# Products by token in groups of 512 columns, with quarter-of-rows weight tiles and one PSUM bank for each block, in one decoder-layer step on Trainium2

## The chip, the cores and the metric

The kernel runs on one core of one Trainium2 chip. The metric is the time of one execution on the device in microseconds, as the median of several runs. The kernel before takes 4701.04 us (median of three runs, 4698.99 to 4721.07 us).

## The reference

One decoder layer is computed for a prompt of 1024 tokens and, with the same weights, for one new token of each of 8 samples. Everything is float32 and the model width is 1024. Cut to what matters here:

```python
proj = h @ w_in                                  # h = RMSNorm(x), (tokens, 1024)
z, xbc, dt_raw, rw, gate_raw = split(proj)       # z: 1024 columns, gate_raw: 2 x 1024
y_ssd  = rmsnorm(SSD(xbc, dt_raw) * silu(z))
y_rwkv = RWKV7(rw)
merged = sigmoid(gate_ssd) * y_ssd + sigmoid(gate_rwkv) * y_rwkv
x = x + merged @ w_out
x = x + CrossAttn(rmsnorm(x)) @ w_mo             # 4 heads, 256 memory tokens
x = x + PEER(rmsnorm(x))                         # 8 heads x top 16 of 16384 one-neuron experts
y = rmsnorm(x)
```

PEER finds, for every token, 8 x 16 experts: scores by `w_pq` and sub-keys, a top 16 of each half, a top 16 of their pairs. Each chosen expert costs a row of 4 KB of `expert_u` (a dot product with the token) and a row of `expert_v` (added with a coefficient).

## The kernel before

**Fronts and experts.** The 1024 prompt tokens go in four groups of two blocks of 128 tokens. All of the layer but the experts' sums is a "front" of a group (`front(gi)`, `gi` 0 to 3; "front 1" to "front 4" in the text). Eight sample rows ride along as a small third block: their input products in front 1, their Z, gate and `w_out` products in front 2, their `w_mo` product and expert choice in front 3. The experts of one group are worked on beside the next front: for each of the 128 choices of a block, POOL gathers 128 rows into a `U` tile (L1512, 512 KB) and DVE takes the dot product (L1516) or adds the row to the sum (L1568). After front 4 come what is left of these, the last group's `u` rows, and a dense sum over `expert_v` for two blocks (matmuls with `cs`, `vs` and `cmat`).

**Order.** A scheduler places the instructions of all engines when the kernel is built. A front's instructions stand ahead of the previous group's experts, which fill in. On the chip each engine runs its own list in that fixed order, and SP issues the loads in a fixed order too, each once its buffer is free.

**Two forms of product.** By channel: weights stationary, tokens moving (`by_channel`). By token: a block's activations stationary (`hT`, `mT`, `oT`: 8 slices of 128 rows), weights moving, the result a block's rows by some columns (`by_token`). The change is about four products by token, each to 1024 columns: Z (L499 on: `w_in` columns, evicted by ACT `Tanh` into an `f2` tile at L507 and by DVE into `mg` at L509, and at L511 and L512 for the sample rows), the SSD gate GS (L847 on: ACT L854, DVE L855), and `project` for `w_out` and `w_mo` (L1042 on: DVE L1053). The RWKV gate GR that follows GS also goes by token and isn't touched. Front 1 does its products in a three-part split for accuracy (`sa`), so its Z and GS aren't touched either; its `project` is, and there `rest` runs once for each block.

**As it is before,** each of the four goes in steps of 256 columns: `weights()` loads two `w` tiles (rows 0 to 511 and 512 to 1023, 512 KB each, in runs of 1 KB), and then for each block a `pp` bank takes 8 matmuls of 256 columns and is evicted before the next but one block can use it. All matmuls are recorded at the helper L112; one float32 matmul of the program leaves two records.

**Buffers.** PSUM has eight banks of 512 columns: `pp` 2, `pc` 2, `pg` 1, `tp` 1, `pv` 2. `pc` is also used by the PEER scores (product of queries and sub-keys, evicted by ACT into one of three `sc` tiles, which DVE's top 16 frees), by the SSD, by the scan and by the attention of the samples. `w` has 5 tiles, `f2` has 4.

**Neighbours.** Z is followed by `dt` and by the 12 convolution channels, GS and GR run beside DVE's triangular inverse (L841 and L843), which the scan needs, and each `project` is followed by an RMSNorm.

Of the kernel before, what the change touches and what calls it, by code (L numbers as in the profile page):

```python
# [13 lines left out]
OP = mybir.AluOpType  # L14
# [30 lines left out]
def decode_layer(ctx, tc, I, O):  # L45
# [289 lines left out]

    kt2_d = dr.tile([2, P, 8, P], F32, name="kt2_d")
# [125 lines left out]
    def front(gi):  # L462
# [36 lines left out]
        for i in range(4):  # L499
            wt = weights(w_in, Z0 + i * 256, split=sa)  # L500
            aside_satt(SATT[0])
            s2 = slice(i * 256, i * 256 + 256)
            for b, (t0, n) in enumerate(body):
                p = pp()
                by_token(wt, hT, t0, n, p)
                th = f2()
                S.activation(th[:n, :256], p[:n, :256], AF.Tanh, scale=0.5)  # L507
                if b < nb:
                    V.scalar_tensor_tensor(mg[b][:n, s2], th[:n, :256], 1.0, p[:n, :256], op0=OP.add, op1=OP.mult)  # L509
                else:  # L510
                    V.scalar_tensor_tensor(th[:n, :256], th[:n, :256], 1.0, p[:n, :256], op0=OP.add, op1=OP.mult)  # L511
                    V.tensor_tensor(mg[b][:n, s2], th[:n, :256], mg[b][:n, s2], op=OP.mult)  # L512
# [334 lines left out]
        for i in range(4):  # L847
            wt = weights(w_in, GS0 + i * 256, split=sa)
            s2 = slice(i * 256, i * 256 + 256)
            for b, (t0, n) in enumerate(body):  # L850
                p = pp()
                by_token(wt, hT, t0, n, p)
                th = f2()
                S.activation(th[:n, :256], p[:n, :256], AF.Tanh, scale=0.5)  # L854
                V.scalar_tensor_tensor(mg[b][:n, s2], th[:n, :256], 1.0, mg[b][:n, s2], op0=OP.add, op1=OP.mult)  # L855
# [178 lines left out]
        def rest(bl):  # L1034
# [7 lines left out]
            def project(w, src, smp_src=None):  # L1042

                for i in range(4):
                    wt = weights(w, i * 256)
                    s2 = slice(i * 256, i * 256 + 256)
                    for b, (t0, n) in enumerate(body):
                        p = pp()
                        if b == nl and smp_src:
                            by_token(wt, smp_src, 0, n, p)  # L1050
                        else:
                            by_token(wt, src, t0, n, p)
                        V.tensor_tensor(mg_[b][:n, s2], p[:n, :256], mg_[b][:n, s2], op=OP.add)  # L1053
# [749 lines left out]
```

## Time and profile before

| | |
|---|---|
| median of three runs | 4701.04 us |
| the profiled execution | 4729.15 us, span 4727.4 us |
| PE busy, DVE busy | 75%, 78% |
| ACT busy, POOL busy | 29%, 53% |
| 16 DMA engines busy | 56.0% gathers, 26.5% all other loads and stores |
| granted TensorE clock, mean | 0.795 of full speed |

Busy times are those of one profiled execution. A window of the trace gives, for a stretch of the span, each engine's busy time, the granted TensorE clock (1.0 is 2.4 GHz, 0.5 is 1.2 GHz) and the busy share of the DMA engines. "[x <-y]" behind a row is the idle time of the engine before it and what ended it. PE busy counts pipelined matmuls and isn't PE at its peak.

### The profile page before, as it was taken

Reading aid. Unit: us, or ns where it says so; the run is one execution under the profiler, and the core shown is the slowest. Engines: PE = TensorE matmul, PEld = TensorE weight load, DVE = VectorE, ACT = ScalarE, POOL = GpSimd, SP = SyncE. Lnnn points to the kernel's source line nnn. Section 1 sums busy time; section 2 is a strip of 40 time slices with the busy share of each in tenths; the row PEclk is TensorE's granted clock in tenths of the full one; section 3 lists DMA queues with packets and bytes.
Section 4 is the critical chain, followed back from the end, with each engine's and each line's share of the span. In section 5 each row is a group of like instructions: output and inputs, shape, how many; then the busy total and the mean of one; then the engine's idle time right before and its main releaser. Section 6 shows DMA issues by size and latency. Waiting matters only on the chain.

```text
span 4727.4 us, 56327 instructions
## 1 busy us (share of the span) xinstructions
PE 3534.4 (75%) x18278; PEld 2706.4 (57%) x18278; DVE 3697.7 (78%) x7765; ACT 1351.2 (29%) x3489; POOL 2501.9 (53%) x2059
## 2 busy tenths in 40 slices
PE   7889875779886786788785884387976885338998
PEld 6778764557565565366574673265655743235555
DVE  5662287998878679988886699888766797998888
ACT  5545322133123221133132221132222215233322
POOL 0000035665656645564666657855545477774664
PEclk9987877888865887788757886588757897559999
DMA  4342588899978998899989987899869878988998
GB/s 123 99 130 73 173 280 318 269 320 344 337 260 283 354 339 275 318 323 318 349 269 353 340 280 272 281 328 312 287 217 357 310 239 312 344 311 326 406 406 352
DMA packets 609103, 1369.20 MB, mean 290 GB/s; under 512 B 86124, under 2 KB 332296, under 8 KB 608800
## 3 DMA queue, kind: packets, MB, share of 16 engines
q0 software_dynamic: 260352, 948.03, 56.0%
q1 hardware_dynamic: 348456, 417.57, 26.5%
q8 instruction: 145, 2.38, 0.2%
q14 instruction: 150, 1.23, 0.1%
HBM read 1335.60 MB, written 29.90 MB: 289 GB/s over the span
## 4 chain that ended last, share of the span: by engine, by line
DVE 32%; PE 30%; DMA 15%; issue 12%; ACT 5%; POOL 5%; SPq 1%; another core or an unknown queue 0%; POOLq 0%; DVEq 0%; ACTq 0%
PE pp L112 16%; DVE U L1516 10%; PE pc L112 8%; DVE acc L1568 5%; POOL U L1512 4%; DMA U<-in_expert_v_dram,idx 4%; DMA U<-in_expert_u_dram,idx 3%; PE pg L112 2%; PE pv L112 2%; DVE q3b L450 2%; DMA w<-in_w_in_dram 1%; PE tp L112 1%; DMA q<-kt_d 1%; DVE vs L1616 1%; DVE f L579 1%
## 5 line engine op out<-in xcount | busy, mean ns | idle before, releaser
L1512 POOL DMA_INDIRECT U<-in_expert_u_dram,idx x1024 | 1298.6, 1268 | 732.4 <-issue 189.8
L1516 DVE CUSTOM_DVE_ANT_0 U<-U,xa 128x1024 f32<-128x1024 f32 x1032 | 1267.9, 1239 | 115.3 <-DMA U<-in_expert_u_dram,idx 106.5
L1512 POOL DMA_INDIRECT U<-in_expert_v_dram,idx x768 | 925.8, 1205 | 724.7 <-DVE acc L1568 183.1
L1568 DVE SCALAR_TENSOR_TENSOR acc<-U,cf,acc 128x1024 f32<-128x1024 f32 x708 | 924.0, 1305 | 98.6 <-DMA U<-in_expert_v_dram,idx 85.1
L112 PE MATMUL pp<-qw,w 128*128 128x256 f32 (+2 forms) x2872 | 745.8, 413 | 151.2 <-issue 40.9
L112 PEld LDWEIGHTS pp<-qw,w 128*128 128x128 f32 x2872 | 591.3, 218 | 277.1 <-issue 110.8
L112 PE MATMUL pp<-w,qw 128*128 128x256 f32 (+1 forms) x2528 | 633.9, 405 | 117.9 <-DVE g L509 30.0
L112 PEld LDWEIGHTS pp<-w,qw 128*128 128x128 f32 (+1 forms) x2528 | 484.5, 195 | 247.2 <-DVE g L509 34.1
L112 PE MATMUL pc<-vs,cs 128*128 128x512 f32 x510 | 200.1, 447 | 35.8 <-ACT vs L118 19.9
L112 PE MATMUL pp<-q,w 128*128 128x128 f32 (+1 forms) x1024 | 196.0, 350 | 16.6 <-DMA w<-in_w_pq_dram 8.8
L112 PEld LDWEIGHTS pp<-q,w 128*128 128x128 f32 x1024 | 169.1, 210 | 33.0 <-ACT q L118 10.5
L121 POOL TENSOR_TENSOR q3b<-q3b,q3b 128x400 f32<-128x400 f32 (+1 forms) x130 | 154.6, 1202 | 57.3 <-DVE q3b L450 55.1
L112 PE MATMUL pp<-vs,cs 128*128 128x512 f32 x510 | 172.9, 393 | 0.0
L112 PE MATMUL pc<-rst,q 64*64 64x64 f32 x1024 | 170.5, 305 | 1.6 <-issue 1.0
L112 PE MATMUL pg<-q,q 64*128 64x128 f32 (+1 forms) x384 | 108.5, 441 | 79.5 <-DMA q<-kt_d 39.9
L304 PE MATMUL tp<-ident,g 128*128 128x128 f32 (+1 forms) x296 | 62.2, 346 | 138.5 <-DVE g L1018 52.2
L112 PE MATMUL pc<-g,q 128*64 128x64 f32 x1024 | 138.8, 316 | 16.2 <-issue 12.4
L112 PEld LDWEIGHTS pc<-vs,cs 128*128 128x128 f32 x510 | 93.5, 188 | 91.0 <-ACT vs L118 36.2
L112 PEld LDWEIGHTS pg<-q,q 64*128 64x128 f32 (+1 forms) x384 | 81.6, 273 | 101.0 <-DMA q<-kt_d 42.6
L112 PE MATMUL pc<-q,q 64*128 64x128 f32 (+1 forms) x512 | 102.1, 343 | 47.7 <-ACT q L118 27.8
L304 PEld LDWEIGHTS tp<-ident,g 128*128 128x128 f32 (+1 forms) x296 | 44.0, 183 | 157.3 <-issue 55.9
L112 PEld LDWEIGHTS pc<-rst,q 64*64 64x64 f32 x1024 | 114.4, 188 | 29.9 <-issue 3.2
(506 smaller groups left out, 6336.6 us busy)
## 6 DMA issues: line engine op xcount, KB each, us to landing
w<-in_w_in_dram SPq DMA_DIRECT2D x248, 512.0 KB
U<-in_expert_v_dram SPq DMA_DIRECT2D x128, 512.0 KB
w<-in_w_pq_dram SPq DMA_DIRECT2D x80, 512.0 KB
w<-in_w_out_dram SPq DMA_DIRECT2D x40, 512.0 KB
w<-in_w_mq_dram SPq DMA_DIRECT2D x40, 512.0 KB
w<-in_w_mo_dram SPq DMA_DIRECT2D x40, 512.0 KB
U<-in_expert_u_dram,idx POOLq DMA_INDIRECT x1024
U<-in_expert_v_dram,idx POOLq DMA_INDIRECT x768
```

The costliest lines, as they stand in the source:

```text
L112: T.matmul(out, a, b, start=first, stop=last)
L121: G.tensor_tensor(out, a, b, op=op)
L304: T.transpose(p[:, j * P:j * P + n], x[:, c * P:(c + 1) * P], ident[:n, :n])
L450: V.tensor_tensor(oh[:n], iota50[:n, None, :].to_broadcast([n, 8, NCAND]), posf[:n, h, k8].unsqueeze(2).to_broadcast([n, 8, NCAND]), op=OP ...
L579: V.scalar_tensor_tensor(acc[:, 3 - k:TP], p[:, :TP - 3 + k], cw(k), acc[:, 3 - k:TP], op0=OP.mult, op1=OP.add)
L1512: G.indirect_dma_start(out=dst, out_offset=None, in_=table, in_offset=bass.IndirectOffsetOnAxis(ap=idx, axis=0))
L1516: V.tensor_tensor_reduce(out=u, in0=u, in1=x, scale=1.0, scalar=0.0, op0=OP.mult, op1=OP.add, accum_out=out)
L1568: V.scalar_tensor_tensor(z["acc"], v, cf, z["acc"], op0=OP.mult, op1=OP.add)
L1616: V.tensor_scalar(rb[:, a, :], iota, by[:, 1, t0 + a:t0 + a + 1], by[:, 2, t0 + a:t0 + a + 1], op0=OP.is_equal, op1=OP.mult)
```

## The change

`wide_by_token` is new. It goes over the weights in four tiles of 256 rows by 512 columns (512 KB, runs of 2 KB), and with each tile does two matmuls of 512 columns for every block; the sums of the blocks stand side by side, one bank for each: `pp` for the first block, `pc` for the second, `pg` for the third. After the fourth tile all blocks are evicted, 512 columns at a time. `project` uses it in all four fronts, Z and GS in fronts 2 to 4.

```diff
+    def wide_by_token(w, c0, body, src, p):
+        for i in range(4):
+            x = wtile().rearrange("p a b -> p (a b)").rearrange("p (k c) -> p k c", k=2)
+            load(x, w[i * 256:(i + 1) * 256, c0:c0 + 512].rearrange("(k p) c -> p k c", p=P))
+            for b, (t0, n) in enumerate(body):
+                for k in range(2):
+                    mm(p[b][:n, :], src(b)[i][:, k, t0:t0 + n], x[:, k, :], i == 0 and k == 0, i == 3 and k == 1)
...
-        for i in range(4):
-            wt = weights(w_in, Z0 + i * 256, split=sa)
-            aside_satt(SATT[0])
-            s2 = slice(i * 256, i * 256 + 256)
-            for b, (t0, n) in enumerate(body):
-                p = pp()
-                by_token(wt, hT, t0, n, p)
-                th = f2()
-                S.activation(th[:n, :256], p[:n, :256], AF.Tanh, scale=0.5)
...
+        def by_512(c0):
+            for i in range(2):
+                ps = [(pp, pc, pg)[b]() for b in range(len(body))]
+                wide_by_token(w_in, c0 + i * 512, body, lambda b: hT, ps)
+                for b, (t0, n) in enumerate(body):
+                    yield b, n, slice(i * 512, i * 512 + 512), ps[b][:n, :]
+        tokens = by_256 if sa else by_512
+        aside_satt(SATT[0])
+        for b, n, s2, p in tokens(Z0):
+            th = f2()[:n, :s2.stop - s2.start]
+            S.activation(th, p, AF.Tanh, scale=0.5)
+            if b < nb:
+                V.scalar_tensor_tensor(mg[b][:n, s2], th, 1.0, p, op0=OP.add, op1=OP.mult)
...
+        for b, n, s2, p in tokens(GS0):
+            th = f2()[:n, :s2.stop - s2.start]
+            S.activation(th, p, AF.Tanh, scale=0.5)
+            V.scalar_tensor_tensor(mg[b][:n, s2], th, 1.0, mg[b][:n, s2], op0=OP.add, op1=OP.mult)
...
             def project(w, src, smp_src=None):
-                for i in range(4):
-                    wt = weights(w, i * 256)
...
+                for i in range(2):
+                    s2 = slice(i * 512, i * 512 + 512)
+                    ps = [(pp, pc, pg)[b]() for b in range(len(body))]
+                    wide_by_token(w, i * 512, cols, lambda b: parts[b], ps)
                     for b, (t0, n) in enumerate(body):
+                        V.tensor_tensor(mg_[b][:n, s2], ps[b][:n, :], mg_[b][:n, s2], op=OP.add)
```

`by_256` is the old loop, kept for front 1. `SATT[0]` is 0, so the moved call does nothing.

## Rows read from the trace of the kernel before

**Rows 1.** The page: engines (us, share, instructions) and DMA queues (packets, MB, share)

```profile
PE 3534.4 (75%) x18278; PEld 2706.4 (57%) x18278; DVE 3697.7 (78%) x7765; ACT 1351.2 (29%) x3489; POOL 2501.9 (53%) x2059
...
q0 software_dynamic: 260352, 948.03, 56.0%
q1 hardware_dynamic: 348456, 417.57, 26.5%
```

**Rows 2.** The page: the chain that ended last, by engine

```profile
DVE 32%; PE 30%; DMA 15%; issue 12%; ACT 5%; POOL 5%; SPq 1%; another core or an unknown queue 0%; POOLq 0%; DVEq 0%; ACTq 0%
```

**Rows 3.** Windows: length, busy us by engine, granted clock, DMA share, GB/s

```profile
1786.00:1872.00 86.00, 55.01 (x219) 45.81 (x219) 82.93 (x253) 12.12 (x27) 53.46 (x46) 0.73 0.81 268
1872.00:2022.00 150.00, 112.17 (x284) 59.54 (x282) 138.56 (x436) 18.80 (x59) 81.40 (x69) 0.75 0.88 315
2767.00:2850.00 83.00, 63.06 (x255) 52.20 (x256) 78.16 (x264) 16.80 (x42) 47.58 (x44) 0.82 0.79 268
2850.00:3002.00 152.00, 49.88 (x141) 36.94 (x140) 144.82 (x418) 19.66 (x47) 117.39 (x85) 0.65 0.80 274
1214.00:1335.00 121.00, 103.33 (x461) 69.21 (x460) 109.31 (x206) 16.80 (x44) 83.17 (x64) 0.90 0.96 347
...
1481.00:1578.00 97.00, 63.76 (x314) 43.74 (x310) 78.14 (x112) 24.35 (x77) 69.29 (x56) 0.79 0.95 341
...
668.00:697.00 29.00, 18.26 (x74) 14.68 (x72) 29.00 (x69) 1.50 (x3) 10.31 (x4) 0.81 0.79 250
```

**Rows 4.** Who waited for whom, whole span: us in total, times, longest

```profile
PE pp L112 <- DVE g L509: 35.9, 14, 6.9
...
PE pp L112 <- ACT f L854: 27.6, 6, 10.3
...
PE pp L112 <- DVE g L1053: 21.9, 10, 4.7
```

**Rows 5.** DVE groups by shape: busy us, mean ns of one, idle before

```profile
L668 DVE TENSOR_TENSOR st<-pp,st 128x512 f32<-128x512 f32 x16 | 10.9, 681 | 0.0
...
L1053 DVE TENSOR_TENSOR g<-pp,g 128x256 f32<-128x256 f32 x64 | 26.8, 420 | 54.8 <-PE pp L112 44.5 <-DMA g<-in_x_prompt_dram 8.1 <-issue 2.1
L509 DVE SCALAR_TENSOR_TENSOR g<-f,pp 128x256 f32<-128x256 f32 x32 | 13.0, 409 | 4.3 <-ACT f L507 4.2
```

**Rows 6.** Timeline of PE: start us, length us, what, records

```profile
683.63 6.62 PE L112 MATMUL pp<-w,qw 128*128 128x256 f32 x16 [3.13 <-DVE g L1053]
...
1786.91 7.07 PE L112 MATMUL pp<-w,qw 128*128 128x256 f32 x32
...
4439.62 0.59 PE L112 MATMUL pp<-U,cmat 128*128 128x512 f32 x1
4440.05 1.02 PE L112 MATMUL pc<-U,cmat 128*128 128x512 f32 x2
```

**Rows 7.** Windows at the start (mostly runs of 1 KB) and at the end (4 KB)

```profile
0.00:250.00 250.00, 204.50 (x1397) 179.56 (x1398) 148.07 (x294) 130.85 (x312) 9.64 (x48) 0.92 0.38 108
...
4500.00:4727.00 227.00, 199.45 (x690) 126.50 (x688) 195.43 (x264) 65.14 (x132) 122.12 (x97) 0.97 0.96 378
```

**Rows 8.** Timeline of PE and ACT: scores of fronts 2 and 3 in `pc`

```profile
1781.40 0.49 PE L112 MATMUL pc<-q,q 128*128 128x128 f32 x2 [0.60 <-ACT gate L456]
...
1870.65 0.38 ACT L118 ACTIVATE sc<-pc 128x256 f32<-128x256 f32 x1 [1.44 <-DVE q3b L424]
...
2849.39 0.37 ACT L118 ACTIVATE sc<-pc 8x256 f32<-8x256 f32 x1 [1.95 <-DVE q3b L424]
```

**Rows 9.** The inverse (fronts 2, 4: first and last start), and GR's last products

```profile
L843 DVE TENSOR_TENSOR g<-g,f x31: 185/354/450, 1255.2 to 1317.5; 128x31 f32<-128x31 f32 x2, 128x60 f32<-128x60 f32 x2, 128x87 f32<-128x87 f32 x2, 128x112 f32<-128x112 f32 x2
...
L843 DVE TENSOR_TENSOR g<-g,f x31: 191/353/426, 3298.5 to 3350.5; 128x31 f32<-128x31 f32 x2, 128x60 f32<-128x60 f32 x2, 128x87 f32<-128x87 f32 x2, 128x112 f32<-128x112 f32 x2
...
1330.58 3.62 PE L112 MATMUL pp<-w,qw 128*8 128x256 f32 x16
...
3346.36 3.62 PE L112 MATMUL pp<-w,qw 128*128 128x256 f32 x16
```

More of the change, by code (lines that the diff above doesn't have):

```diff
@@ L497, in aside_satt, with by_256 @@
                 next(satt)
-        for i in range(4):
-            wt = weights(w_in, Z0 + i * 256, split=sa)
-            aside_satt(SATT[0])
-            s2 = slice(i * 256, i * 256 + 256)
-            for b, (t0, n) in enumerate(body):
-                p = pp()
-                by_token(wt, hT, t0, n, p)
-                th = f2()
-                S.activation(th[:n, :256], p[:n, :256], AF.Tanh, scale=0.5)
[L508 to L512, printed above, removed]
+        def by_256(c0):
+            for i in range(4):
+                wt = weights(w_in, c0 + i * 256, split=True)
+                for b, (t0, n) in enumerate(body):
+                    p = pp()
+                    by_token(wt, hT, t0, n, p)
+                    yield b, n, slice(i * 256, i * 256 + 256), p[:n, :256]
+        def by_512(c0):
+            for i in range(2):
+                ps = [(pp, pc, pg)[b]() for b in range(len(body))]
+                wide_by_token(w_in, c0 + i * 512, body, lambda b: hT, ps)
+                for b, (t0, n) in enumerate(body):
+                    yield b, n, slice(i * 512, i * 512 + 512), ps[b][:n, :]
[6 more added lines that the diff above has]
+                V.scalar_tensor_tensor(mg[b][:n, s2], th, 1.0, p, op0=OP.add, op1=OP.mult)
+            else:
+                V.scalar_tensor_tensor(th, th, 1.0, p, op0=OP.add, op1=OP.mult)
+                V.tensor_tensor(mg[b][:n, s2], th, mg[b][:n, s2], op=OP.mult)
         dtt = t("dtt", [P, 4, 16], 2)
@@ L1042, in project @@
             def project(w, src, smp_src=None):
-                for i in range(4):
-                    wt = weights(w, i * 256)
-                    s2 = slice(i * 256, i * 256 + 256)
-                    for b, (t0, n) in enumerate(body):
[L1048 to L1053, printed above, removed]
+                parts = [smp_src if b == nl and smp_src else src for b in range(len(body))]
+                cols = [(0 if b == nl and smp_src else t0, n) for b, (t0, n) in enumerate(body)]
+                for i in range(2):
+                    s2 = slice(i * 512, i * 512 + 512)
+                    ps = [(pp, pc, pg)[b]() for b in range(len(body))]
+                    wide_by_token(w, i * 512, cols, lambda b: parts[b], ps)
+                    for b, (t0, n) in enumerate(body):
+                        V.tensor_tensor(mg_[b][:n, s2], ps[b][:n, :], mg_[b][:n, s2], op=OP.add)
             mT = [qw() for _ in range(4)]
```

8 lines of the change are left out of this document (removed).

## The prediction

> **What bounds the kernel now.** I read the page first. No engine is full: DVE 78%, PE 75%, and the two DMA queues together hold the 16 DMA engines for 82.5% of the span [rows 1]. The chain of waits is spread in the same way, DVE 32%, PE 30%, DMA 15% [rows 2]: the bound changes from stage to stage. So I cut windows around the four changed products [rows 3]. Two kinds appear. Around GS and GR (1214 to 1335) and `w_out` (1481 to 1578) the DMA engines are busy for 0.96 and 0.95: gathers and weights fill them. Where Z runs in fronts 3 and 4, with the convolutions behind it (1786 to 2022, 2767 to 3002), DVE is busy for 82.93 of 86.00, 138.56 of 150.00, 78.16 of 83.00 and 144.82 of 152.00 us, 92 to 96%, because the last front's top 16 and the experts run beside the new front. Only front 1, which has few experts beside it yet, is held by its own chain of products and evictions; in its window (668 to 697) DMA is at 0.79, and PE works 18.26 of 29.00 us. In the first kind a PE that waits less mostly leaves the transfers as they are, in the second it leaves DVE as it is. That decides how much of each saving below I count.
>
> **The change part by part.** It covers Z and GS in fronts 2 to 4 (7 blocks each) and `project` in all fronts (9 blocks for `w_out`, 9 for `w_mo`): 32 blocks by 1024 columns.
>
> *PE's columns: nothing.* 32 records of 256 columns take 7.07 us; with the last one's tail as long as in the single row below (0.59 less the pitch of 0.43, so 0.16), that is (7.07 - 0.16) / 32 = 0.216 us each. Two more records of 512 columns lengthen a run from 0.59 to 1.02, 0.43 for the second [rows 6]. Twice 0.216 is 0.43: half the weight loads go, but they lay under the matmuls. Bounds: 0, and 0.002 x 1024 new records, 2 us. I take 0.
>
> *Loads: -8 us.* 128 loads stay 128 of 512 KB, 67.1 MB, in runs of 2 KB instead of 1 KB. The gather queue (4 KB rows) takes 0.560 x 4727.4 / 948.03 = 2.79 us of all 16 engines for a MB, the other queue, mostly 1 KB, 0.265 x 4727.4 / 417.57 = 3.00 [rows 1]. If 2 KB came as cheap as the gathers, 67.1 x 0.21 = 14 us. The farthest rows give more: 0.38 x 250 / 27.0 = 3.52 us for a MB in the first window and 0.96 x 227 / 85.8 = 2.54 in the last [rows 7], so at most 67.1 x 0.98 = 66; the least is 0, as a run of twice the length isn't dearer by the byte in any row. I take 14, as those rows are of whole queues. Only 72 of the 128 loads (GS, and `project` of fronts 2 to 4) lie where DMA is full: 14 x 72 / 128 = 8. By the Trainium skill ("DMA: Bandwidth & Descriptors", "Why small descriptors are slow") each packet has some three cycles beside one cycle for 32 bytes: 67 instead of 70 cycles for 2 KB, an estimate of 4% or 9 us of the 201 that 67.1 MB cost, and 5 of them counted; the rows lie above that.
>
> *Fewer evictions: -5 us.* DVE's 132 operations of 256 columns become 66 of 512. One of 256 takes 0.409 to 0.420 us, one of 512 out of PSUM 0.681 [rows 5]: 66 x (0.84 - 0.68) = 10 us of DVE time. Bounds 0 and 10; DVE is full for about half of the windows, so 5. ACT's 56 `Tanh` become 28; at 29% [rows 1] that is worth 0.
>
> *PE's waits for evictions.* Before, a block's bank must be evicted before the next but one product. After, a step of 512 uses one `pp` and one `pc` of two each, so all four sums of a two-block front fit without a wait; only the third block meets its own `pg` again. PE's waits are 35.9 us for L509, 27.6 for L854 and 21.9 for L1053 [rows 4]. What each is worth:
> - `project` in front 1: three of these waits, 7.5 us (one is the 3.13 in [rows 6]). Nothing runs beside it, so they count; four last evictions get 0.26 longer. -6 us, bounds 0 and -8.
> - `project` in fronts 2 to 4: 14.4 us. Against it, both blocks now end together: before, the first block's last eviction and the squares for the norm lay under 16 records of the other, 3.46 us, now under two of 512, 0.86. That costs up to 2.6 us six times; I take 0.7 each, as one of the two squares still runs beside the other eviction. 14.4 - 4 = 10, half of it since DMA is full: -5 us, bounds +2 and -14.
> - GS: 13.0 us in front 2 and 13.6 in front 4. In front 4 the inverse ends at 3350.5 and GR's last products at 3346.36 + 3.62 = 3350.0 [rows 9]: DVE is late as well, so 0. In front 2 the inverse is done at 1317.5 and the products at 1334.2, so 13 us could be saved; DMA is at 0.96 there, so half: -6 us, bounds 0 and -27.
> - Z: about 30 us in fronts 2 to 4, gone or turned into the next term.
>
> *A new wait: Z needs `pc`: +8 us.* Before, Z used `pp` alone and so could start while PEER's scores of the front before still held both `pc` banks: a score product of front 2 ends at about 1781.9 [rows 8], Z of front 3 starts at 1786.91 [rows 6], and the last score leaves `pc` at 1871.0; in the next front the last one leaves it at 2849.8 [rows 8], with Z at the head of the window from 2767 [rows 3]. The scores come first in the order, so Z's second block, and with it every later PE instruction of that front (dt, the convolutions' products), may wait until then: 84 and some 82 us, 166 in all. ACT's evictions of the scores wait for DVE's top 16, which this doesn't slow. What covers it is DVE, 92 to 96% busy there: the experts and the top 16 still fill it, and the evictions taken from the front of these stretches come behind them. The bounds are -30 (Z's waits gone, `pc` free in time) and +166; the cover leaves at most the DVE idle time of these windows to grow, 26.5 us before, and I take +8, near the row of DVE.
>
> *Beside these*, a tile of weights is now free after 2 instead of 4 slices, so SP, whose later loads queue behind each wait, gets a little further ahead; not counted.
>
> Sum: -8 - 5 - 6 - 5 - 6 + 8 = -22 us on the profiled execution, 4729.15 us (span 4727.4). That one lies 28 us over the median of 4701.04; as none of the terms hangs on what made it longer, I take the 22 off the median: 4679 us.
>
> **The rivals.**
> - *The waits count in full.* If the front's chain is the bound and experts only fill in, the 85 us of [rows 4], less 4 in front 1's untouched Z and 4 for ends, and 14 of loads all come off: 4701 - 91 = 4610 us. For it: PE has 30% of the chain. Against: full DMA and DVE in [rows 3]. Chance 0.15.
> - *Z is held by the scores* (slower). If DVE runs dry while Z waits, half of the 166 us shows: 4701 + 83 - 30 = 4754 us. It decides from the point at which more than about 30 us of the delay is uncovered. For it: the last scores of [rows 8], and in-order PE. Against: DVE's share. Chance 0.20.
> - *Nothing shows.* Experts and gathers set the pace, and the front finishes when they do: 4701 +/- 10 us. Chance 0.08.
> - *The clock falls.* If turning between banks made PE look less busy, its clock would fall in these products: 16 records then take 6.62 instead of 3.5 us [rows 6], so at most 442 us (2048 records before, at 0.216) more, and a third of that on the path, about 4850 us. The dense sum at the end turns through four banks at a granted clock of 0.97 [rows 7], which speaks against it. The Trainium skill ("TensorE: Matmul & The Clock Gate", "A second HAM failure mode: psum-queue depth-cycling") tells of a kernel whose clock swung for just this reason; by that rule 4850, by the row no change. Chance 0.03.
>
> **How the numbers follow.** The forecast, 4679 us, has 0.54; its own range is 4655 to 4703. About 0.5%, 23.5 us, is what a measurement of this kernel can tell from no change, so the forecast lies at the edge of faster (4677.5): 0.26 of its chance is faster, 0.28 the same. With the rivals: faster 0.26 + 0.15 = 0.41, same 0.28 + 0.08 + 0.02 of the held Z = 0.38, slower 0.18 + 0.03 = 0.21. The range for 8 in 10 reaches into both large rivals, 4615 to 4760.
>
> **What the profile after would show.** Right: L1053, L509 and L855 in 512 columns at about 0.68 us, half as many; PE's waits for them near none; the loads' queue with some 33 thousand fewer packets and under 26.5%. Z of fronts 3 and 4 starting tens of us after the last `w_pq` product, with DVE still over 90% busy there, would show the new wait and its cover. Wrong: DVE share falling in these windows (the held Z), or span saved near the sum of all PE waits (the first rival). The scheduler places everything anew, so shifts of some 10 us in stages that the change doesn't touch would blur all of this.

## The result and the profile after

The kernel after takes 4781.03 us (median, 4777.86 to 4807.44), the kernel before, run on the same chip, 4704.32 us: a ratio of 1.0151, with an interval of 1.0124 to 1.0179. It is slower by 1.5%, 21 us above the upper end of my range. The profiled execution took 4782.52 us, of which 4780.7 are its span, 53.3 more than the span before. The profiled execution before lies 25 us above its median, so the two profiles show 53 of the 77 us between the medians.

The page after, against [rows 1] and [rows 2]: engines with busy us, share and instructions; two DMA queues; the chain by engine.

```profile
PE 3476.0 (73%) x17254; PEld 2474.6 (52%) x17254; DVE 3697.7 (77%) x7699; ACT 1347.9 (28%) x3462; POOL 2518.0 (53%) x2059
...
q0 software_dynamic: 260352, 948.03, 55.1%
q1 hardware_dynamic: 315688, 417.57, 25.8%
...
PE 31%; DVE 29%; DMA 18%; issue 11%; ACT 5%; POOL 4%; another core or an unknown queue 1%; SPq 1%; POOLq 0%; DVEq 0%; ACTq 0%
```

The edits did what they say: 1024 matmul records fewer, 66 operations of DVE fewer, 32,768 packets fewer in the second queue. DVE's busy time is the same to the tenth, so the 53 us are time in which DVE waits. The page doesn't tell where. For that I cut every front at the same events, read from the timelines of PE and DVE: the last product of `w_pq`, the last operation of the convolutions, the last product by channel for the RWKV part, the end of the scan (PE's last record that reads the state `rst`), the last eviction of `w_mo`. The lengths of the stretches between them add up to the span:

| stretch (us) | before | after | difference |
|---|---|---|---|
| start to the end of front 1 | 862.0 | 850.7 | -11.3 |
| Z, `dt`, convolutions, front 2 | 157.1 | 147.9 | -9.2 |
| Z, `dt`, convolutions, fronts 3 and 4 | 480.3 | 541.4 | **+61.1** |
| SSD and products by channel, fronts 2 to 4 | 627.7 | 610.3 | -17.4 |
| GS, GR, inverse, scan, fronts 2 to 4 | 840.5 | 887.3 | **+46.8** |
| end of the scan to the end of `w_mo`, fronts 2 to 4 | 587.0 | 572.4 | -14.6 |
| from there to the last `w_pq` product, fronts 2 to 4 | 252.9 | 246.6 | -6.3 |
| after front 4 | 919.9 | 924.2 | +4.3 |

Two stretches lose 108 us, the others together win 55. By fronts, the first loser is 39.6 us longer in front 3 and 21.5 in front 4, the second 17.7 and 42.6 in fronts 2 and 3 and 13.4 shorter in front 4. The first loser on PE's timeline of the kernel after, in front 3 (columns as in [rows 6]):

```profile
1792.15 8.75 PE L112 MATMUL pp<-w,qw 128*128 128x512 f32 x20
1814.23 7.01 PE L112 MATMUL pp<-wdt,qw 128*128 128x16 f32 x32 [13.32 <-DVE g L530]
1852.23 2.08 PE L112 MATMUL pg<-triu,adt 128*128 128x128 f32 x8 [30.99 <-DVE adt L562]
1854.10 2.25 PE L112 MATMUL pc<-q,q 128*128 128x128 f32 x12
1865.87 10.50 PE L112 MATMUL pc<-w,qw 128*128 128x512 f32 x20 [9.52 <-ACT sc L118]
1876.20 1.88 PE L112 MATMUL pp<-w,qw 128*128 128x512 f32 x4
```

The first block's sum starts with the front, as in [rows 6]. The second block's stands 74 us behind it, after the last scores, and starts when ACT has evicted one of them. Z ends at 1886.7 instead of 1830.4 us, and the convolutions' products come behind it. PE's idle 31 us for `adt`, the end of the `dt` chain on DVE, lie in the same time: that product stands ahead of the last scores in PE's list. In front 4 the second block starts at 2918.03, after the scores too, 80 us behind the first.

The second loser, on the same timeline a little later. `tp<-sel,q`, the transposes at L806 and `tp<-q,q` are the small products of the last quarter of the RWKV heads; `tp<-q,q` makes the input of the triangular inverse.

```profile
2267.33 1.22 PE L112 MATMUL pp<-q,k 64*128 64x256 f32 x2 [0.56 <-ACT q L782]
2268.48 7.15 PE L112 MATMUL pc<-w,qw 128*128 128x512 f32 x12
2275.46 5.31 PE L112 MATMUL pp<-w,qw 128*128 128x512 f32 x12
2280.61 0.95 PE L112 MATMUL tp<-sel,q 128*128 128x4 f32 x8
2281.42 1.96 PE L112 MATMUL pp<-w,qw 128*128 128x512 f32 x4
...
2288.37 0.38 PE L806 MATMUL tp<-ident,q 128*128 128x128 f32 x2
...
2296.63 0.68 PE L112 MATMUL tp<-q,q 64*64 64x64 f32 x16
2297.24 1.13 PE L112 MATMUL pp<-w,qw 128*128 128x512 f32 x2
2298.20 1.88 PE L112 MATMUL pc<-w,qw 128*128 128x512 f32 x4
2300.01 0.68 PE L112 MATMUL tp<-q,q 64*64 64x64 f32 x16
```

All 64 records of GS (`pc<-w,qw`, `pp<-w,qw`, 512 columns) stand ahead of the last small product, which runs 32 us after the first record of GS. The inverse starts at 2327.6, 66.5 us after the last product by channel (2261.1); before, at 2260.2, it was 44.9 us. DVE's timeline of the kernel after and, below the dots, of the kernel before:

```profile
2327.38 0.20 DVE L862 TENSOR_TENSOR f<-g,g 128x31 f32<-128x31 f32 x1 [11.75 <-DMA g<-in_rwkv_ln_w_dram]
2327.62 0.21 DVE L864 TENSOR_TENSOR g<-g,f 128x31 f32<-128x31 f32 x1
...
2260.20 0.21 DVE L843 TENSOR_TENSOR g<-g,f 128x31 f32<-128x31 f32 x1
```

The windows of the kernel after that answer to [rows 3]: Z and the convolutions of fronts 3 and 4, and GS of front 3.

```profile
1792.00:1887.00 95.00, 41.16 (x119) 23.78 (x118) 91.69 (x313) 13.57 (x21) 52.28 (x46) 0.68 0.70 228
1887.00:2068.00 181.00, 118.30 (x324) 61.13 (x323) 160.89 (x405) 22.07 (x73) 111.90 (x91) 0.77 0.93 338
2838.00:2940.00 102.00, 46.06 (x147) 26.50 (x145) 98.49 (x278) 14.24 (x38) 81.67 (x67) 0.70 0.91 320
2940.00:3104.00 164.00, 64.86 (x197) 49.01 (x198) 139.83 (x381) 21.37 (x56) 114.07 (x83) 0.70 0.77 266
2261.00:2328.00 67.00, 47.16 (x155) 24.95 (x154) 44.09 (x71) 10.33 (x23) 38.55 (x34) 0.82 0.98 361
```

While Z waits DVE is indeed busy, 91.69 of 95 and 98.49 of 102 us, 96 to 97%. Its gaps lie behind: 160.89 of 181 and 139.83 of 164 us, 89 and 85% in the convolutions, which had 92 and 95% [rows 3]. What ended them, in the second and in the fourth window (us in total, times, longest):

```profile
DVE acc L1582 <- DMA U<-in_expert_v_dram,idx: 7.3, 8, 2.4
DVE f L600 <- ACT halo L118: 5.8, 2, 4.6
DVE U L1530 <- DMA U<-in_expert_u_dram,idx: 4.2, 7, 1.0
...
DVE U L1530 <- DMA U<-in_expert_u_dram,idx: 14.8, 11, 4.1
DVE f L600 <- ACT halo L118: 5.1, 1, 5.1
```

DVE waits there for gathered expert rows, 11.5 of 20 and 14.8 of 24 us (before, 3.4 of 11 and 4.0 of 7), and for the convolutions' own steps. That the experts' work at hand was used up during the wait for Z fits this; it isn't shown further.

In the last window, that of GS, DVE is busy for 44 of 67 us; its longest wait, 11.75 us, is the one that ends with the inverse's start. DMA is at 0.98 there; in the stretch that answers to it before (2215 to 2260) it was at 0.96.

### The profile page after: what moved, and what is told of

Same layout as the page of the kernel before. It is cut to its first block, busy times and chain, and to the rows that moved or that the text cites. A ratio compares the mean times of both kernels' runs of the same rounds, so it can differ in the third digit from the quotient of the medians.

```text
span 4780.7 us, 54127 instructions
## 1 busy us (share of the span) xinstructions
PE 3476.0 (73%) x17254; PEld 2474.6 (52%) x17254; DVE 3697.7 (77%) x7699; ACT 1347.9 (28%) x3462; POOL 2518.0 (53%) x2059
## 4 chain that ended last, share of the span: by engine, by line
PE 31%; DVE 29%; DMA 18%; issue 11%; ACT 5%; POOL 4%; another core or an unknown queue 1%; SPq 1%; POOLq 0%; DVEq 0%; ACTq 0%
PE pp L112 16%; DVE U L1530 9%; PE pc L112 8%; DVE acc L1582 4%; DMA U<-in_expert_u_dram,idx 4%; DMA U<-in_expert_v_dram,idx 4%; POOL U L1526 3%; PE pv L112 2%; PE pg L112 2%; DMA w<-in_w_in_dram 2%; DMA q<-kt_d 2%; PE tp L112 1%; DVE q3b L459 1%; DVE vs L1630 1%
## 5 line engine op out<-in xcount | busy, mean ns | idle before, releaser
L1526 POOL DMA_INDIRECT U<-in_expert_u_dram,idx x1024 | 1320.4, 1289 | 736.5 <-issue 208.1
L112 PE MATMUL pp<-qw,w 128*128 128x256 f32 (+2 forms) x2872 | 731.9, 407 | 164.5 <-DVE f L600 50.7
L112 PEld LDWEIGHTS pp<-qw,w 128*128 128x128 f32 x2872 | 578.5, 213 | 288.4 <-issue 119.7
L112 PE MATMUL pp<-w,qw 128*128 128x256 f32 (+2 forms) x1056 | 391.7, 504 | 38.3 <-DMA w<-in_w_out_dram 10.5
L112 PEld LDWEIGHTS pp<-w,qw 128*128 128x128 f32 (+1 forms) x1056 | 201.4, 197 | 187.5 <-issue 114.6
L121 POOL TENSOR_TENSOR q3b<-q3b,q3b 128x400 f32<-128x400 f32 (+1 forms) x130 | 142.9, 1114 | 149.3 <-DVE q3b L459 147.9
L112 PE MATMUL pp<-q,w 128*128 128x128 f32 (+1 forms) x1024 | 196.9, 351 | 11.3 <-DMA w<-in_w_pq_dram 9.1
L112 PE MATMUL pc<-w,qw 128*128 128x512 f32 x384 | 185.7, 617 | 13.6 <-ACT sc L118 10.1
L112 PEld LDWEIGHTS pc<-w,qw 128*128 128x128 f32 x384 | 75.0, 199 | 107.6 <-issue 92.7
```

What stands on the lines that cost most here:

```text
L112: T.matmul(out, a, b, start=first, stop=last)
L121: G.tensor_tensor(out, a, b, op=op)
L1526: G.indirect_dma_start(out=dst, out_offset=None, in_=table, in_offset=bass.IndirectOffsetOnAxis(ap=idx, axis=0))
```

## The experiments

Theories: **A**, wide Z waits because its second bank `pc` is held by the scores. **B**, wide GS runs ahead of the inverse's inputs on the in-order engines. Rivals: **C**, Z's 512-column form costs by itself; **D**, wide GS costs wherever it stands. A third question came up on the way: what makes `project` faster. Ratios are to the kernel before in the same set of runs; its median was 4667 to 4716 us in the sets used, so times of different sets aren't compared.

All kernels at a glance. "Z" is the stretch of fronts 3 and 4, "GS to scan" and "project" those of fronts 2 to 4, as in the table above, from one profiled execution each, and these too come from different sets.

| kernel | ratio (95% interval) | front 1 ends | Z | GS to scan | project |
|---|---|---|---|---|---|
| before | 1 | 862.0 | 480.3 | 840.5 | 587.0 |
| after | 1.0151 (1.0124 to 1.0179) | 850.7 | 541.4 | 887.3 | 572.4 |
| `z256` | 1.0075 (1.0051 to 1.0099) | 851.2 | 501.3 | 864.2 | 554.5 |
| `gs256` | 1.0042 (1.0027 to 1.0058) | 856.7 | 546.0 | 795.5 | 564.4 |
| `zgs256` | **0.9898** (0.9881 to 0.9914) | 856.3 | 488.3 | 812.9 | 543.1 |
| `z_pv` | 1.0141 (1.0124 to 1.0158) | 858.8 | 529.8 | 884.8 | 554.6 |
| `z_pg` | 0.9986 (0.9968 to 1.0004) | 862.9 | 476.8 | 823.9 | 562.0 |
| `gs_tp_z256` | 1.0001 (0.9982 to 1.0019) | 850.9 | 484.9 | 840.2 | 545.9 |
| `gs_pp_z256` | 0.9982 (0.9960 to 1.0003) | 851.2 | 480.0 | 842.0 | 560.8 |
| `gs_hold` | 1.0039 (1.0017 to 1.0060) | 852.5 | 502.4 | 889.1 | 564.2 |
| `gs_hold_nt` | 1.0065 (1.0044 to 1.0085) | 858.9 | 487.3 | 859.5 | 554.7 |
| `z_pg_gs_tp` | 1.0081 (1.0049 to 1.0112) | 856.2 | 479.5 | 861.1 | 556.1 |
| `z_pg_gs_hold` | 1.0035 (1.0017 to 1.0053) | 856.1 | 489.7 | 887.6 | 561.6 |
| `z_pg_gs_hold_nt` | 0.9991 (0.9974 to 1.0008) | 862.8 | 482.8 | 855.4 | 550.7 |
| `proj_1kb` | 1.0016 (1.0000 to 1.0032) | 849.5 | 482.1 | 789.6 | 582.6 |
| `proj_2x1kb` | 0.9909 (0.9877 to 0.9940) | 835.0 | 468.8 | 831.9 | 568.8 |
| `proj_n2kb` | 1.0019 (1.0000 to 1.0038) | 857.6 | 497.1 | 823.1 | 618.6 |

One caution for all of it: each edit makes the scheduler place every instruction anew. Kernels whose Z goes in 256 columns have 469 to 502 us in that column, kernels with GS in 256 columns 790 to 841 in theirs. So a difference of 30 us in Z or of 50 us in "GS to scan" between two single kernels can't be read, and a group that lies clear of another can. The totals scatter too. The same step, Z from 256 columns to 512 with `pg` (`z_pg` and the three whose names begin with it), costs 0.88% beside GS in 256 columns and 0.80% beside `gs_tp_z256`, and gives back 0.04% beside `gs_hold` and 0.74% beside `gs_hold_nt`. A total that differs from one neighbour's by less than some 0.9% doesn't show a cause by itself, and no kernel was run that only places the instructions anew.

### Parts of the change undone

`z256`: Z goes by the old loop in all fronts, GS and `project` stay wide. (In every kernel that uses the old loop in fronts 2 to 4, `split=True` in it becomes `split=sa`.)

```diff
-        for b, n, s2, p in tokens(Z0):
+        for b, n, s2, p in by_256(Z0):
```

> Z of fronts 2 to 4 goes back to steps of 256 columns in pp alone; GS and project stay wide. Theory A (wide Z waits for the two pc banks that PEER's scores of the front before hold): Z of fronts 3 and 4 starts at once behind the last w_pq product again, some 75 us earlier than in the changed kernel, and the time falls by 40 to 55 us, to 4725 to 4740. Theory B (the loss is made by wide GS, whose products stand ahead of the inverse's inputs on PE): at most 10 us come back, 4770 or more. Theory C (wide products cost wherever they stand, through the order in which everything is placed): a part by the share of Z, some 20 us, 4760.

Measured: 1.0075, 0.76% or 36 us back, a little less than A expected and more than C. The Z stretch falls from 541 to 501 us.

`gs256`: the same edit at `tokens(GS0)`; Z and `project` stay wide.

> GS of fronts 2 to 4 goes back to steps of 256 columns in pp alone; Z and project stay wide. Theory B: the inverse of fronts 2 to 4 starts 17 to 24 us earlier behind the last product of the RWKV channels, and 25 to 50 us come back, 4730 to 4755. Theory A alone: less than 10 us come back, 4770 or more, and Z of fronts 3 and 4 still starts some 75 us late. Theory C: some 20 us, 4760.

Measured: 1.0042, 1.09% or 51 us back, the upper end of what B expected. "GS to scan" falls from 887 to 796 us.

`zgs256`: both, so only `project` is wide.

> Z and GS of fronts 2 to 4 both go back to 256 columns; project alone is wide, in all fronts. Theories A and B together: all of the loss comes back and project's own gain shows, 4685 to 4705, level with or a little under the kernel before. If A and B are each only part of it and the wide form costs by itself (C), it stays over 4735. The prediction's own step for project was -11 us with its loads.

Measured: 0.9898, 47 us faster than before, where I expected 0 to 20. Of the three parts of the change one is worth 1%, and the other two together cost 2.5%.

PE's timeline of `zgs256`, at the place of the second loser above: 32 records of 256 columns of GS stand ahead of the last `tp<-q,q`, which runs 13 us after the last `pp<-q,k` (33 in the kernel after). The two `pp` banks are then full, and the next sum has to wait for ACT.

```profile
2206.02 0.70 PE L112 MATMUL pp<-q,k 64*128 64x256 f32 x2 [0.56 <-ACT q L782]
2206.65 1.13 PE L112 MATMUL pc<-k,q 128*128 128x256 f32 x4
2207.61 7.07 PE L112 MATMUL pp<-w,qw 128*128 128x256 f32 x32
2214.52 0.95 PE L112 MATMUL tp<-sel,q 128*128 128x4 f32 x8
...
2219.36 1.09 PE L112 MATMUL tp<-q,q 64*64 64x64 f32 x16 [0.47 <-ACT f L118]
...
2227.83 3.72 PE L112 MATMUL pp<-w,qw 128*128 128x256 f32 x16 [1.87 <-ACT f L870]
```

### Another bank for wide Z

`z_pv`: all three products wide, Z's second block in the two banks of `pv`.

```diff
+            two = pv() if c0 == Z0 else None
             for i in range(2):
-                ps = [(pp, pc, pg)[b]() for b in range(len(body))]
+                ps = [(pp, pc, pg)[b]() if b != 1 or two is None else two[:, i * 512:i * 512 + 512]
+                      for b in range(len(body))]
```

> As the changed kernel, but the second block's two banks of wide Z are the two banks of pv, which the scores don't use, in place of pc. Same products, loads and evictions. Theory A: as with narrow Z, Z of fronts 3 and 4 starts behind the last w_pq product, 4720 to 4740. If it isn't the bank but the wide form of Z (C), it stays within 10 us of 4781. Theory B: 4770 or more.

Measured: 1.0141, no better than after (1.0151). That would speak for C, or for B alone, but for the timeline of PE in front 3:

```profile
1789.77 7.03 PE L112 MATMUL pp<-w,qw 128*128 128x512 f32 x16
1797.98 1.95 PE L112 MATMUL pp<-w,qw 128*128 128x512 f32 x4 [1.18 <-DMA w<-in_w_in_dram]
...
1878.59 10.03 PE L112 MATMUL pv<-w,qw 128*128 128x512 f32 x16 [10.48 <-DVE acc L1549]
```

`pv` is held there as well, by the final norm of a finished block (L1549, which reads it), until 1878. The experiment had put one held bank in the place of another and tells nothing of A or C by its total. In front 4, where `pv` was free, the stretch is 235.8 instead of 265.3 us.

`z_pg`: GS in 256 columns; in fronts 3 and 4, where there is no third block, the second takes `pg`.

```diff
+                two = pg if c0 == Z0 and len(body) == 2 else pc
-                ps = [(pp, pc, pg)[b]() for b in range(len(body))]
+                ps = [(pp, two, pg)[b]() for b in range(len(body))]
```

> Z in groups of 512 as in the change, but in fronts 3 and 4 the second block's sum goes to the bank pg, which neither the scores nor the experts' sums hold; GS back in 256 columns. Beside it stand the same kernel with pc (4690.77 us, 1.0042 of before) and with Z in 256 columns too (0.9898). Theory A (Z waits because its second bank is held by the scores; which bank it is, is all that matters): 0.988 to 0.994 of before, at least two thirds of the 67 us between those two come back, and Z of fronts 3 and 4 ends within some 50 us of the last product of w_pq instead of 100. Rival C (it is the wide Z itself, what its 512-column form does to the order and the weight tiles): 1.000 to 1.006, as with pc.

Measured: 0.9986. The stretch is as A says, 476.8 us against 546.0 with `pc` and 488.3 in 256 columns, and Z of front 3 runs straight behind `w_pq`:

```profile
1771.76 1.89 PE L112 MATMUL pp<-q,w 128*128 128x256 f32 x8
1773.48 1.88 PE L112 MATMUL pg<-w,qw 128*128 128x512 f32 x4
1775.20 3.60 PE L112 MATMUL pp<-w,qw 128*128 128x512 f32 x8
```

So A holds for the place of the loss: the four kernels with `pg` have 477 to 490 us there, the two with `pc` 541 and 546. The total took only 0.56% of the 1.44% between the two neighbours, between A and C. The profiled execution is 28 us slower than this kernel's median and shows no single place: against `gs256` the products by channel are 20 and "GS to scan" 28 us longer, the latter within the scatter. The four pairs in the caution above show no price of an early Z that holds throughout; whether there is one here is open.

### Where wide GS may stand

`gs_tp_z256`: Z in 256 columns, GS wide; its first step takes `tp`, which the small products need before it.

```diff
+                one = tp if c0 == GS0 and i == 0 else pp
-                ps = [(pp, pc, pg)[b]() for b in range(len(body))]
+                ps = [(one, pc, pg)[b]() for b in range(len(body))]
```

> GS in groups of 512 as in the change, but its first step takes the bank tp, which the small products that feed the triangular inverse use before it, so GS can't stand in front of them; Z back in 256 columns. Beside it stand the same kernel with pp in that step (4706.09 us, 1.0075 of before) and with GS in 256 columns too (0.9898). Theory B (wide GS with four free banks runs ahead on PE of what the inverse needs): 0.988 to 0.996, and the inverse of fronts 3 and 4 starts at most 40 us after the last product of its front by channel, instead of 66. Rival D (wide GS costs because its weight loads or its evictions get in the way, wherever it stands): 1.004 to 1.010.

Measured: 1.0001, under half of the way, and the inverse starts only 1 to 7 us earlier than in `z256`. Only the first block's first sum was kept back: 24 records of the second block and of the second step still stand ahead (40 in front 2).

`gs_hold`: the first weight tile of GS is touched by one copied element that hangs on the inverse's loaded input, so no product of GS and no load behind that tile can stand ahead.

```diff
+            if hold is not None and i == 0:
+                V.tensor_copy(x[:1, 0, 0:1], hold)
             load(x, w[i * 256:(i + 1) * 256, c0:c0 + 512].rearrange("(k p) c -> p k c", p=P))
...
-        for b, n, s2, p in tokens(GS0):
+        for b, n, s2, p in (by_256(GS0) if sa else by_512(GS0, sn[:1, 0, 0:1])):
```

> Z in 256 columns; GS in groups of 512 with the change's own banks (pp, pc), but its first weight tile is first touched by a one-element copy from the tile sn, the inverse's input: so no product of GS and none of its later loads behind that tile can stand ahead of what the inverse needs, on PE or on SP. Beside it: the same without the hold (z256, 1.0075 of before), with tp as first bank (gs_tp_z256, 1.0001, where the second block's products and the second step still went ahead), and with GS in 256 columns (zgs256, 0.9898). Theory B (wide GS runs ahead of the inverse's inputs): from the last product by channel to the inverse's start 40 to 48 us in fronts 3 and 4, as with GS in 256 columns, instead of 58 to 67; in total 0.985 to 0.995. Rival D (wide GS costs wherever it stands): the start comes earlier, but the stretch from there to the end of the scan gets as much longer; 1.000 to 1.008.

Measured: 1.0039. `gs_hold_nt` hangs the same copy on the last small product's evicted tile, some 25 us earlier (`nt[:1, 0:1]` for `sn[:1, 0, 0:1]`).

> As gs_hold (Z in 256 columns, GS in groups of 512 in its own banks), but the one-element copy that holds back GS's first weight tile reads the last small product that feeds the inverse (its evicted tile nt) and not the inverse's loaded input: GS may start some 25 us earlier than in gs_hold. There the stretch to the inverse's start was as short as with GS in 256 columns, but GR, which follows GS, fell into the scan, which got 15 to 45 us longer. Theory B (order alone: wide GS costs only by standing ahead of what the inverse needs or by pushing GR past it): 0.988 to 0.997 of before, from the last product by channel to the end of the scan in fronts 2 to 4 together 800 to 835 us, as in the kernels with GS in 256 columns (790 to 832). Rival D (wide GS costs wherever it stands): 1.001 to 1.006, and 850 us or more.

Measured: 1.0065, with 859.5 us in "GS to scan". Both kernels are above what B expected, and by the totals and this stretch (850 or more) D would stand. The parts tell more. Front 3, in us after its last product by channel, from the timelines of PE, ACT and DVE:

| kernel | GS records ahead of the last small product | that product | inverse starts | inverse ends | last eviction of GR | scan ends |
|---|---|---|---|---|---|---|
| before | 32 of 256 | 23.5 | 44.9 | 100.6 | 101.4 | 258.9 |
| `zgs256` | 32 of 256 | 17.5 | 43.8 | 96.4 | 97.2 | 251.1 |
| after | 64 of 512 | 39.6 | 66.5 | 138.3 | 98.2 | 301.4 |
| `z256` | 64 of 512 | 33.8 | 65.5 | 138.3 | 96.5 | 290.8 |
| `gs_tp_z256` | 24 of 512 | 22.0 | 58.3 | 123.5 | 85.7 | 275.4 |
| `gs_pp_z256` | 32 of 512 | 26.8 | 50.0 | 110.1 | 98.1 | 272.2 |
| `gs_hold` | none | 22.3 | 49.0 | 96.6 | 124.0 | 266.1 |
| `gs_hold_nt` | none | 22.1 | 55.2 | 105.4 | 109.6 | 277.3 |

The scan needs the inverse, and GS with GR is the other work of the stretch. Before, both end together in front 3. Wide GS brings the inverse's end 38 us later, 22 by its start and 16 by a longer run (72 instead of 56 us), and its own end hardly earlier: 98 against 101 us. DMA is full there in both, at 0.98 and 0.96, which fits; no run tests it. Held, the inverse is in time and GR ends some 25 us late, into the scan. On SP's timeline of `gs_hold_nt` five weight loads of GS still stand ahead of the load of the inverse's input:

```profile
2220.92 31.51 SPq L851 DMA_DIRECT2D nd<-f  x32
2252.53 2.96 SPq L342 DMA_DIRECT2D w<-in_w_in_dram  x5
2256.98 1.71 SPq L858 DMA_DIRECT2D g<-nd  x1
```

There the inverse starts 33.1 us after the last small product, in `gs_hold` 26.7.

The other fronts have the same order but not the same price. In front 2 the inverse ends after 138.6 instead of 109.9 us, GR after 124.9 instead of 126.8, and the scan 17.7 us later. In front 4 the inverse starts after 67.6 instead of 43.5 us, but takes 38.5 instead of 52.2; the scan, counted from the later end of inverse and GR, takes 165 instead of 187 us, so that it ends 13 us earlier, counted from the last product by channel. Why these two got shorter isn't shown.

`gs_pp_z256`: GS wide, both blocks in `pp`, so that the second step waits for the evictions of the first.

```diff
-                ps = [(pp, pc, pg)[b]() for b in range(len(body))]
+                ps = [(pp, pp if c0 == GS0 else pc, pg)[b]() for b in range(len(body))]
```

> Z in 256 columns; GS in groups of 512 with both blocks' sums in the two pp banks, as before the change, so that its second step must wait for the evictions of the first, and with the change's quarter-of-rows tiles. The same with pp and pc: 1.0075. If the four free banks let GS run ahead (my reading of theory B): 0.990 to 0.999, and 42 to 52 us from the last product by channel to the inverse's start in fronts 3 and 4. If it is the loads of the eight tiles, which stand ahead of the inverse's stores on SP whatever the banks: 1.003 to 1.009, and 57 us or more.

Measured: 0.9982. Half as many records go ahead, the inverse starts at 50.6, 50.0 and 49.3 us in fronts 2 to 4, where `z256` has 61.2, 65.5 and 66.8. So the four free banks let GS run ahead, as B says; the loads alone, on the same tiles, don't. What remains against `zgs256` is 0.8%, and 29 us in "GS to scan", both within the scatter; in front 3 the inverse still ends 12 us after GR, and takes 60 us instead of 53 beside the wider products. How much of it is order and how much D is open.

### Both mends together

`z_pg_gs_tp`, `z_pg_gs_hold` and `z_pg_gs_hold_nt` have all three products wide and put `z_pg`'s edit together with one of those above.

> All products of the change in groups of 512, with both banks exchanged as in the two kernels beside it (Z's second block in pg in fronts 3 and 4, GS's first step in tp). If A and B are the whole loss: 0.985 to 0.995 of before, 120 us below the change itself (1.0151). If the form of 512 columns has a cost of its own in Z or GS: 1.000 or more.

> Everything of the change in groups of 512, Z's second block in pg in fronts 3 and 4 and GS held as in the kernel beside it. If A and B are the whole loss of the change and hold mends B: 0.985 to 0.996; if the two mends together only move work to where DVE is late, as the two with tp did (1.0081): 1.002 or more.

> All products of the change in groups of 512, Z's second block in pg in fronts 3 and 4 and GS held as in gs_hold_nt. If both waits are the whole loss: within 0.4% of gs_hold_nt, and 0.988 to 0.997 where theory B holds there; if wide Z has a cost that comes back later, as its total with narrow GS (0.9986) may mean: 1.000 to 1.006.

Measured: 1.0081, 1.0035 and 0.9991. The first two came out where a cost of the wide form itself, or work moved to where DVE is late, was expected. The Z stretch is short in all three. The best takes back 1.6% and stands where the kernel before is; it is below `gs_hold_nt` (1.0065), outside the 0.4% that I gave. No wide form of Z and GS that I found beats 256 columns.

### What makes project faster

All three have Z and GS in 256 columns. `proj_1kb` has `project`'s wide banks and wide evictions, with the old weight tiles (512 rows by 256 columns, runs of 1 KB).

```diff
-                    wide_by_token(w, i * 512, cols, lambda b: parts[b], ps)
+                    for hf in range(2):
+                        wt = weights(w, i * 512 + hf * 256)
+                        for b, (t0, n) in enumerate(cols):
+                            by_token(wt, parts[b], t0, n, ps[b][:, hf * 256:hf * 256 + 256])
```

> Only project is changed (Z and GS as before): its banks, products' order and evictions as in the change as far as the bank goes (one bank of 512 columns a block, one eviction of 512), but the weights are loaded as before, in tiles of 512 rows by 256 columns with runs of 1 KB. The same kernel with quarter-of-rows tiles and runs of 2 KB has 0.9898 of before, 47 us less. If banks and evictions bring it (my terms for them were 11 us, for project's loads 4 to 5): 0.990 to 0.993. If the loads bring it (longer runs, tiles free after a quarter): 0.997 to 1.000.

Measured: 1.0016. PE's waits for `project`'s evictions fell from 21.9 to 2.8 us, and the time didn't: the banks and the wide evictions, for which I had counted 11 us, bring nothing that can be measured.

`proj_2x1kb` has the change's quarter-of-rows tiles, each loaded by two transfers with runs of 1 KB.

```diff
-            load(x, w[i * 256:(i + 1) * 256, c0:c0 + 512].rearrange("(k p) c -> p k c", p=P))
+            for hf in range(2):
+                h2 = slice(hf * 256, hf * 256 + 256)
+                load(x[:, :, h2], w[i * 256:(i + 1) * 256, c0 + hf * 256:c0 + hf * 256 + 256].rearrange("(k p) c -> p k c", p=P))
```

> As zgs256 (only project wide, 0.9898) with the same quarter-of-rows tiles, freed after each quarter, but each tile loaded by two transfers of 256 KB with runs of 1 KB. If the length of the runs brings project's gain: 0.997 to 1.002, as with tiles of 512 rows and 1 KB (proj_1kb, 1.0016). If the tile's shape does (freed after a quarter, so that loads start earlier): 0.988 to 0.993.

Measured: 0.9909, the same as `zgs256` with runs of 2 KB (0.9898). The length of the runs made no difference here that the intervals, 0.2 and 0.3% to either side, can tell.

`proj_n2kb` has runs of 2 KB, but 256-column sums in `pp`, and the four tiles of a step held until its second half:

```diff
+                    xs = []
+                    for k in range(4):
+                        x = wtile().rearrange("p a b -> p (a b)").rearrange("p (k c) -> p k c", k=2)
+                        load(x, w[k * 256:(k + 1) * 256, i * 512:i * 512 + 512].rearrange("(k p) c -> p k c", p=P))
+                        xs.append(x)
+                    for hf in range(2):
...
+                        for b, (t0, n) in enumerate(body):
+                            p = pp()
...
+                            for k in range(8):
+                                mm(p[:n, :256], parts[b][k // 2][:, k % 2, c0_:c0_ + n], xs[k // 2][:, k % 2, hf * 256:hf * 256 + 256], k == 0, k == 7)
...
```

> As before, but project's weights come in quarter-of-rows tiles with runs of 2 KB; its sums stay 256 columns wide in the two pp banks, evicted 256 columns at a time, and the four tiles of a step are held until its second half. If the length of the runs alone brings project's gain: 0.988 to 0.994. If the wide banks or the early freeing of tiles are needed: 0.997 or more.

Measured: 1.0019, with 618.6 us in "project", the longest of all. So the gain goes with the change's tiles, which are done with after two slices, and with the order of products that belongs to them and never needs more than one tile for all blocks. The columns "front 1 ends" and "project" added up say the same, though with little to spare: 1397 to 1425 us in the fourteen kernels with these tiles, 1432, 1449 and 1476 in `proj_1kb`, the kernel before and `proj_n2kb`.

How the tiles bring it isn't shown. SP's timeline at `w_out` of front 3, in `zgs256`:

```profile
2481.21 4.40 SPq L340 DMA_DIRECT2D w<-in_w_out_dram  x3
2488.14 19.23 SPq L254 DMA_DIRECT2D w<-in_w_mq_dram  x5
```

and in the kernel before:

```profile
2512.87 0.36 SPq L1534 DMA_DIRECT2D out_dram<-acc  x1
2513.27 0.43 SPq L254 DMA_DIRECT2D w<-in_w_out_dram  x1
2515.25 0.56 SPq L254 DMA_DIRECT2D w<-in_w_out_dram  x1
2519.52 0.38 SPq L254 DMA_DIRECT2D w<-in_w_out_dram  x1
2519.99 20.76 SPq L254 DMA_DIRECT2D w<-in_w_mq_dram  x5
```

Counted from the end of the scan (2454.1 and 2474.2), the first of the last three `w_out` tiles is issued after 27 instead of 39 us, `w_mq` after 34 instead of 46, and `w_out`'s last eviction comes after 48.0 instead of 66.6. But SP waited for different things there, in `zgs256` for PE to be done with a tile, and before for DVE (us in total, times, longest):

```profile
SPq L340 <- PE pc L112: 19.7, 3, 16.4
...
SPq L1534 <- DVE g L1053: 48.9, 1, 48.9
```

Before, the loads stood in SP's list behind the store of a finished block (L1534), which waited for that block's final norm on DVE (the row names another operation of DVE; the norm's last one, L1533, ends at 2512.8); in `proj_1kb` such a store held SP for 48.3 us. In `zgs256` the store is through at 2460.8. So this row compares places of a store as well as tiles. In `proj_2x1kb`, as fast in total, the three distances are 34, 41 and 61.7 us, and in front 4 `zgs256` has 33, 39 and 57.3 against 29, 41 and 55.8 before. Whether the tile that comes free sooner or the new placement brings the gain is open.

## Why the prediction was wrong

Two steps failed: Z's wait for `pc`, which I named, bounded at +166 and took as covered, and GS, whose term had no bound on the slow side. A third, `project`, came out larger than its terms.

- **PE's columns, 0:** holds. PE has 1024 records fewer, and its mean granted clock is 0.798, before 0.795. The rival "the clock falls" is out with it. What the Trainium skill tells of a kernel that turned between PSUM banks ("TensorE: Matmul & The Clock Gate", "A second HAM failure mode: psum-queue depth-cycling") isn't seen in that row.
- **Loads, -8:** the packets came as forecast, and the queue's share is 19 us of the 16 engines smaller (0.258 x 4780.7 = 1233 against 0.265 x 4727.4 = 1253), near the 14 (the rounding of the shares allows 5 either way). In time nothing of it could be told between `zgs256` and `proj_2x1kb`, which test it for `project`.
- **Fewer evictions, -5:** right in size, with 0.67 to 0.69 us for 512 columns, but not seen in time by itself; DVE's other operations took as much more, as its total stayed.
- **`project`, -6 in front 1 and -5 after it:** too small. `project` alone makes the kernel 1.0% faster, 47 us (`zgs256`). The waits at the banks that the terms were made of aren't the reason: without them `proj_1kb` gains nothing. The gain goes with the tiles, so the sentence that a tile is free after 2 instead of 4 slices, "not counted", may hold it; the way isn't shown. For front 1 the premise "nothing runs beside it" isn't what its row says, as DVE is busy for 29.00 of 29.00 us in the window from 668 [rows 3]. Front 1 gained 11 us in the kernel after and 6 in `zgs256`, but ends between 835 and 863 in the fourteen kernels with these tiles, so that term can't be read.
- **GS, -6:** the stretch from its products to the end of the scan got 47 us longer. I asked which waits of PE fall away, and not what those waits had held back. Two banks in 256 columns let GS go 32 records ahead of the small products; four in 512 let all of it go ahead in fronts 3 and 4. The waits for L854 [rows 4] looked like a loss, and were what kept the order. I even had the row that both chains end together, the inverse at 3350.5 and GR at 3350.0 [rows 9], and read from it only that a faster GS gains nothing there, not that a later inverse can cost. It cost 42.6 us in front 3 and 17.7 in front 2; in front 4, where that row was read, the inverse ended later too, but the stretch got 13.4 us shorter.
- **Z needs `pc`, +8, bounds -30 and +166:** the wait is there, 74 and 80 us, and the stretches of fronts 3 and 4 are 61 us longer. The step that failed is the cover. I took DVE's share in the windows of [rows 3] for room. DVE stayed at 96 to 97% during the wait, as I said it would, but with work that isn't the front's; the front's own convolutions came after it, with DVE at 89 and 85% and waiting in the main for gathered rows. Idle time in the four windows rose from 26.5 to 51 us (3.3, 20.1, 3.5 and 24.2), and the next stretch is 17 us shorter; but `zgs256`, without the wait, has that one 36 us shorter, so this can't be called time given back. Cover by work that has to be done sooner or later only helps where that work, and not the front, ends last.
- **The rivals:** "Z is held by the scores" was the right mechanism, at 0.20 and 4754 us, and its point of 30 us uncovered was passed. The other half of the loss had no rival. "Nothing shows" and "the waits count in full" fell with the result, the latter for `project`'s waits with `proj_1kb` too.

Of the 1.5%, `z256` takes back 0.76 and `gs256` 1.09, both together 2.53, more than the sum; the 0.7 between is left without a cause, and is no more than the totals scatter.

## What to carry to other kernels

A wait at a small number of PSUM banks also limits how far one product may run ahead on an in-order engine: before removing it, list what stands behind it in the queue and who needs that first. Ask of every bank that a product newly takes who holds it at that moment, and price the wait by the front's own chain, not by how busy another engine is with other work. Where loads queue for tiles, test the cut of the tiles apart from banks and runs: here it was the one of the three that the gain went with. And before a timeline is read as a wait for a tile, look at what stands ahead of the load in its queue.

## What the runs showed of the hardware

`project`'s weights in runs of 1 KB or 2 KB made no difference in time that could be told (0.9909 and 0.9898), though the second has half the packets for these loads. The same kernel before took 4667 to 4716 us, as medians of the sets of runs; the two ends bear the same chip number, so what makes this 1% isn't shown, and such a difference can only be read within one set.
